# Filter layer of a Hyena block: two matmul passes on both partition halves, magnitude sums on TensorE, half of the spectrum sums on VectorE

## The chip, the cores and the metric

The kernel runs on one core of a Trainium2 chip. The metric is device time in microseconds of one execution, lower is better. Before the change three executions took 3139.27, 3143.67 and 3150.66 us; the median is 3143.67 us.

## What is computed

One inference step of a two-layer network for 1024 latent tokens and 128 context tokens, model width 1024: layer 0 is differential attention, layer 1 a bidirectional Hyena long convolution, each followed by a SwiGLU feed-forward part. The change touches only the filters of the long convolution, which don't depend on the tokens:

```python
def implicit_filter(L, w1, b1, w2, b2, w3, b3, freq):
    ...
    hdn = jnp.sin(fr * (z @ w1.astype(f32) + b1.astype(f32)))
    hdn = jnp.sin(fr * (hdn @ w2.astype(f32) + b2.astype(f32)))
    h = (hdn @ w3.astype(f32) + b3.astype(f32)).reshape(L, 2, D_MODEL)
    ...
    h = h * jnp.exp(-t[:, None, None] * deltas)
    return h / (jnp.sum(jnp.abs(h), axis=(0, 1), keepdims=True) + FILT_EPS)
```

`z` are 33 features of each position, the hidden width is 64, and `h` holds a forward and a backward filter for each of the 1024 channels. The convolution is done through spectra; the filter's own spectrum is computed by matmuls with a table of cosines and sines. Everything is float32.

## The kernel before

Matmuls take operands of a reduced float32 type. To keep float32 accuracy an operand x is split into a high part, x rounded to that type (a copy on ScalarE), and a low part, x minus the high part (a subtraction). `three` (L304) then adds three products: high x high, high x low, low x high. Its matmuls are lines L305, L306 and L307, and nearly every matmul of the kernel has one of these lines; so the profile tells them apart by tiles. In the same way `tt` (L1248) is the line of most elementwise operations, on VectorE or, if told so, on GpSimd (POOL in the profile).

**filters (L1280)** runs first, before the attention layer. It loads the features and small weights on SyncE's queue, makes two sine layers (`sine`, L1264, seven VectorE instructions, then Sin on ScalarE), and gets `hid`: 64 hidden rows and a row of ones for the bias, by 1152 positions (1024 + 128). L1322 and L1323 split it into `hids`, high and low. The table of cosines and sines is loaded and split next (`forward_table`). Then a loop goes over 8 channel tiles of 128 channels. In it stand side by side the spectrum of tile ct, the filter in time of tile ct + 1, the weights of tile ct + 2, and a few steps of unrelated work (`start` and `early_ada`: adaLN weights from DRAM with one-row matmuls at L368, and the normalisation of the input in three chunks, the results being `hh` and `hl`). When the loop is done, the projection of the attention layer (`qk`, L544) begins.

**filter_weights (L1356)** loads decay tables and the 65 x 2 x 128 weights of a tile (64 rows and a bias row, forward and backward), forms their sum and difference on GpSimd (L1367, L1368), and splits them (ScalarE L1369, GpSimd L1370) into `wh` and `wl` (tiles wsh and wsl in the profile).

**filter_time (L1373)** makes the filter of 9 position blocks: three matmuls each of 65 rows by 256 columns into `mm` banks of PSUM, then VectorE multiplies by the decay into `filt`. For the sum of magnitudes ScalarE takes absolute values (L1399, L1400), VectorE the larger of the two (L1402, since |a + b| and |a - b| have max |a| + |b|), then a TENSOR_REDUCE over the 8 blocks (L1403), and two one-column matmuls against a vector of ones (L1408) sum over partitions. Row 0 of the filter is repaired on GpSimd (L1414, L1415; tile nsq, then filt). `hilo` splits the filter into the operands of the spectrum (ScalarE L1393, VectorE L1394 by way of L1249; the tiles share the names wh and wl).

**filter_spectrum (L1423)** is called twice for a tile. Four matmul groups (`dft`, L1351, with the table th, tl) give PSUM banks; ScalarE copies one operand to SBUF, VectorE makes four sums and differences `f` with one operand in PSUM, and GpSimd four sums and differences `K` of 256 columns from `f` (L1444 to L1447; both tiles are called bf). K goes to DRAM.

The order of instructions on each engine is not the program's: a list scheduler with a cost model orders them when the kernel is built, within the dependences. `issue_after` (L1326, L1334) holds ScalarE's instructions of the block behind the last Sin.

Of the kernel before, what the change touches and what calls it, by code (L numbers as in the profile page):

```python
# [9 lines left out]
F32 = mybir.dt.float32  # L10
F32R = mybir.dt.float32r
AF = mybir.ActivationFunctionType
ALU = mybir.AluOpType
AX = mybir.AxisListType
ENG = mybir.EngineType

P = 128
# [4 lines left out]
NT = LS + LP  # L22
# [83 lines left out]
SUB = HALF // 2  # L106
# [44 lines left out]
class Net:  # L151
# [1096 lines left out]
    def tt(self, o, a, b, op, eng=None):  # L1248
        (eng or self.nc.vector).tensor_tensor(out=o, in0=a, in1=b, op=op)  # L1249
# [30 lines left out]
    def filters(self):  # L1280
        nc, i, sp = self.nc, self.i, self.sp
        H, N = NT // 2, NT // 4
        w1 = self.tl(sp, [33, 64], tag="fw1")
        w2 = self.tl(sp, [P, 64], tag="fw2")
        vec = self.tl(sp, [P, 3], tag="fvec")
        zf = self.htile([33, NT])
        nc.sync.dma_start(zf, i["k_zfeat"])
        nc.sync.dma_start(w1, i["fw1"])
        for r in (0, 64):
            nc.sync.dma_start(w2[r : r + 64], i["fw2"])  # L1290
            nc.sync.dma_start(vec[r : r + 64], i["fvec"])
        hid = self.tl(sp, [65, NT], tag="filt", bufs=2)
        nc.vector.memset(hid[64:65], 1.0)
        mid = self.tl(sp, [P, H], tag="bf", bufs=3)
        cols = [slice(N * q, N * q + N) for q in range(2)]
        xs = []
        for q, c in enumerate(cols):
            ps = self.aux()
            for r in (0, 64):
                nc.tensor.matmul(  # L1300
                    ps[r : r + 64, :N], w1, zf[:, H * (r // 64) + N * q :][:, :N], start=True, stop=True, tile_position=(0, r)
                )
            xs.append(self.sine([ps[:, :N]], vec, 0))
        for c, x in zip(cols, xs):
            mark = nc.scalar.activation(mid[:, c], x, AF.Sin)
        xs = []
        for c in cols:
            halves = []
            for r in (0, 64):
                ps = self.mm()  # L1310
                nc.tensor.matmul(
                    ps[0:64, :N], w2[r : r + 64], mid[r : r + 64, c], start=True, stop=True, tile_position=(r, 0)
                )
                halves.append(ps[0:64, :N])
            xs.append(self.sine(halves, vec, 1))
        for c, x in zip(cols, xs):
            for k in range(2):
                mark = nc.scalar.activation(hid[0:64, H * k + c.start : H * k + c.stop], x[:, N * k : N * k + N], AF.Sin)
        hids = [self.tl(sp, [65, NT], F32R, tag="hid" + n) for n in "hl"]
        for q in range(2):  # L1320
            c = slice(H * q, H * q + H)
            nc.scalar.activation(hids[0][:, c], hid[:, c], AF.Copy)  # L1322
            nc.vector.tensor_tensor(out=hids[1][:, c], in0=hid[:, c], in1=hids[0][:, c].bitcast(F32), op=ALU.subtract)  # L1323
        self.forward_table(sp, sp, "filt")
        self.d_w = [self.tl(self.dp, [P, 2, P], F32, f"d_w{c}") for c in range(KT)]
        with self.tc.issue_after(mark.ins):  # L1326
            w = [self.filter_weights(0), self.filter_weights(1)]
        cur = self.filter_time(0, hids, w.pop(0))
        rest, ada = self.start(), self.early_ada()
        next(rest)  # L1330
        for _ in cur:
            pass
        for ct in range(KT):
            with self.tc.issue_after(mark.ins):  # L1334
                for _ in range(PACE):
                    next(rest, None)
            z = self.zs
            if ct + 2 < KT:
                w.append(self.filter_weights(ct + 2))
            nxt = self.filter_time(ct + 1, hids, w.pop(0)) if ct + 1 < KT else iter(())  # L1340
            next(nxt, None)
            for _ in range(AHEAD.count(ct)):
                next(ada, None)
            self.filter_spectrum(ct, 0, *z[0])
            next(nxt, None)
            self.filter_spectrum(ct, 1, *z[1])
            next(nxt, None)
        for _ in rest:
            pass
# [6 lines left out]
    def filter_weights(self, ct):  # L1356
        nc, i, sp, tt = self.nc, self.i, self.sp, self.tt
        dec = self.tl(self.wp, [P, 8, P], tag="raw", bufs=2)
        nc.sync.dma_start(dec, i["k_decay"][ct][:, 0:LS].rearrange("p (a c) -> p a c", a=8))
        decp = self.tl(self.np_, [P, P], tag="ndg", bufs=2)  # L1360
        nc.sync.dma_start(decp, i["k_decay"][ct][:, LS : LS + P])
        w3 = self.tl(sp, [65, 2, P], tag="w3", bufs=2)
        nc.sync.dma_start(w3, i["fw3"][ct])
        wsd = self.tl(sp, [65, 2, P], tag="wsd", bufs=1)
        wh = self.tl(sp, [65, 2, P], F32R, tag="wsh", bufs=2)
        wl = self.tl(sp, [65, 2, P], F32R, tag="wsl", bufs=2)
        tt(wsd[:, 0], w3[:, 0], w3[:, 1], ALU.add, nc.gpsimd)  # L1367
        tt(wsd[:, 1], w3[:, 0], w3[:, 1], ALU.subtract, nc.gpsimd)  # L1368
        nc.scalar.activation(wh, wsd, AF.Copy)  # L1369
        tt(wl, wsd, wh.bitcast(F32), ALU.subtract, nc.gpsimd)  # L1370
        return dec, decp, wh, wl

    def filter_time(self, ct, hid, w):  # L1373
        nc, i, sp, tt = self.nc, self.i, self.sp, self.tt
        ADD, SUB, MUL = ALU.add, ALU.subtract, ALU.mult
        dec, decp, wh, wl = w
        filt = self.tl(sp, [P, 9, 2, P], tag="filt", bufs=2)
        for a0 in range(0, 9, 2):
            m = min(2, 9 - a0)
            ps = self.mm()  # L1380
            for a in range(m):
                out = ps[:, 256 * a : 256 * a + 256].rearrange("p (f c) -> p f c", f=2)
                t = slice(P * (a0 + a), P * (a0 + a) + P)
                self.three(out, hid[0][:, t], hid[1][:, t], wh, wl)
            d = dec[:, a0 : a0 + m] if m == 2 else decp.unsqueeze(1)
            tt(filt[:, a0 : a0 + m], ps[:, : 256 * m].rearrange("p (a f c) -> p a f c", a=m, f=2), d.unsqueeze(2).to_broadcast([P, m, 2, P]), MUL)
        sm = self.tl(sp, [P, 2, P], tag="fsum", bufs=1)
        self.zs = []

        def hilo(part):  # L1390
            zh = self.tl(self.wp, [P, 8, P], F32R, tag="wh", bufs=3)
            zl = self.tl(self.wp, [P, 8, P], F32R, tag="wl", bufs=3)
            nc.scalar.activation(zh, filt[:, 0:8, part], AF.Copy)  # L1393
            tt(zl, filt[:, 0:8, part], zh.bitcast(F32), SUB)  # L1394
            self.zs.append((zh, zl))

        am = self.tl(self.wp, [P, 8, P], tag="wh", bufs=3)
        am2 = self.tl(self.wp, [P, 8, P], tag="wl", bufs=3)
        nc.scalar.activation(am, filt[:, 0:8, 0], AF.Abs)  # L1399
        nc.scalar.activation(am2, filt[:, 0:8, 1], AF.Abs)  # L1400
        yield
        tt(am, am, am2, ALU.max)  # L1402
        nc.vector.tensor_reduce(out=sm[:, 0], in_=am.rearrange("p a c -> p c a"), axis=AX.X, op=ADD)  # L1403
        nc.scalar.activation(am2[:, 0:2], filt[:, 8], AF.Abs)
        tt(sm[:, 1], am2[:, 0], am2[:, 1], ALU.max)
        ps = self.aux()
        for g in range(2):
            nc.tensor.matmul(ps[:, g : g + 1], sm[:, g], self.ones[:, 0:1], start=True, stop=True)  # L1408
        den = self.den[:, ct]
        nc.vector.tensor_scalar(out=den, in0=ps[:, 0:2], scalar1=FILT_EPS, scalar2=None, op0=ADD)  # L1410
        nc.vector.reciprocal(den, den)
        row = filt[0:1].rearrange("p (u a) f c -> p u a f c", u=1)[:, 0, 0:9:8]
        t = self.tl(self.np_, [1, 2, P], tag="nsq", bufs=2)
        tt(t, row[:, :, 0], row[:, :, 1], ADD, nc.gpsimd)  # L1414
        nc.gpsimd.tensor_scalar(  # L1415
            out=row, in0=t.unsqueeze(2).to_broadcast([1, 2, 2, P]), scalar1=0.5, scalar2=1.0, op0=MUL, op1=MUL
        )
        nc.scalar.dma_start(self.d_w[ct], filt[:, 8])
        hilo(0)
        yield  # L1420
        hilo(1)

    def filter_spectrum(self, ct, part, zh, zl):  # L1423
# [17 lines left out]
        X1 = X1.rearrange("p (a b) -> p a b", a=2)  # L1441
        tt(f[:, 2], X1[:, part], s[:, part], ADD)
        tt(f[:, 3], X1[:, 1 - part], s[:, 1 - part], SUB)
        tt(K[:, 0], f[:, 0], f[:, 2], ADD, nc.gpsimd)  # L1444
        tt(K[:, 2], f[:, 0], f[:, 2], SUB, nc.gpsimd)
        tt(K[:, 1], f[:, 1], f[:, 3], SUB if part else ADD, nc.gpsimd)
        tt(K[:, 3], f[:, 1], f[:, 3], ADD if part else SUB, nc.gpsimd)  # L1447
        nc.scalar.dma_start(self.d_f[ct][:, part], K)
# [300 lines left out]
```

## Time and profile before

| | |
|---|---|
| median of three timed runs | 3143.67 us |
| profiled execution | 3150.18 us, span of the instructions 3148.3 us |
| TensorE busy, share of the span | 3051.0 us, 97% |
| VectorE | 1901.2 us, 60% |
| ScalarE | 1171.4 us, 37% |
| GpSimd | 962.2 us, 31% |
| stretch of the filters, until the first matmul of the projection | 182.4 us |

PE is TensorE's matmuls, PEld its weight loads, DVE VectorE, ACT ScalarE, POOL GpSimd, SP SyncE; a q behind the name is the engine's queue for DMAs. A row of a group gives line, engine, operation, out<-in tiles, shapes, count, then busy time, the mean duration of one in ns, and the idle time of the engine just before with what ended it. Matmuls are pipelined, so durations of neighbours overlap and the distance between their starts says more. PEclk is the granted clock of TensorE.

### The profile page before, as it was taken

To read this page: it belongs to the slowest core of one execution; us is meant where nothing else is said; L and a number is where in the kernel's file an instruction comes from. 1 tells how busy PE (TensorE), PEld (TensorE's weight loads), DVE (VectorE), ACT (ScalarE), POOL (GpSimd) and SP (SyncE) were. 2 spreads that over 40 slices of the span, in tenths; PEclk is the share of its full clock that TensorE was granted. 3 is DMA by queue.
4 is the path that set the end of the run, shared out by engine and by line. 5 is a ranking of instruction groups with operands and counts; after the bars stand their busy time and mean duration, and the time that the engine had idled before them with its cause. 6 is when DMAs were issued, how large, how long until landed. Compare 5 with 4: busy or idle time off the path is not lost. (4 is left out here: it accounts for less than half of the span.)

```text
span 3148.3 us, 53347 instructions
## 1 busy us (share of the span) xinstructions
PE 3051.0 (97%) x21418; PEld 2977.4 (95%) x21418; DVE 1901.2 (60%) x3111; ACT 1171.4 (37%) x2248; POOL 962.2 (31%) x842
## 2 busy tenths in 40 slices
PE   6899999999999999999999999999999999999998
PEld 5779989999999999999999999999999999999998
DVE  7866523888836645445544678886456454445555
ACT  3631123888825322222211443335643222222114
POOL 5744310444422434343000322221223343430003
PEclk9899999999999999999999999999999999999999
DMA  6665352433241222224555223345621212225311
GB/s 250 202 215 186 135 162 82 98 88 90 57 152 55 73 74 74 74 74 148 194 205 193 101 96 123 130 149 181 214 77 57 77 71 77 75 73 199 107 63 67
DMA packets 164494, 379.14 MB, mean 120 GB/s; under 512 B 17391, under 2 KB 80247, under 8 KB 161560
## 3 DMA queue, kind: packets, MB, share of 16 engines
q1 hardware_dynamic: 148872, 353.37, 34.1%
q10 hardware_dynamic: 13968, 17.65, 1.6%
q0 software_dynamic: 1408, 4.72, 0.4%
q8 instruction: 169, 2.77, 0.4%
q14 instruction: 77, 0.63, 0.1%
HBM read 278.94 MB, written 96.73 MB: 119 GB/s over the span
## 5 line engine op out<-in xcount | busy, mean ns | idle before, releaser
L306 PE MATMUL mm<-hs,wh 128*128 128x384 f32 x1632 | 548.2, 336 | 0.4 <-POOL hs L469 0.3
L307 PE MATMUL mm<-hs,wl 128*128 128x384 f32 x1632 | 546.6, 335 | 0.0
L305 PE MATMUL mm<-hs,wh 128*128 128x384 f32 x1632 | 545.9, 336 | 0.0
L863 DVE SCALAR_TENSOR_TENSOR xk<-mm,ada,xk 128x192 f32<-128x192 f32 (+3 forms) x560 | 233.2, 453 | 333.5 <-PE mm L307 328.1
L1249 DVE TENSOR_TENSOR xk<-pr,xk 128x576 f32<-128x576 f32 x200 | 150.7, 754 | 391.9 <-PE pr L307 205.9
L420 POOL TENSOR_TENSOR nacc<-nacc,nsq 128x384 f32<-128x384 f32 x104 | 118.3, 1138 | 682.4 <-ACT nsq L416 680.8
L306 PEld LDWEIGHTS mm<-hs,wh 128*128 128x128 f32 x1632 | 306.4, 188 | 4.7 <-issue 2.2
L305 PEld LDWEIGHTS mm<-hs,wh 128*128 128x128 f32 x1632 | 306.1, 188 | 3.5 <-DVE xk L863 1.8
L307 PEld LDWEIGHTS mm<-hs,wl 128*128 128x128 f32 x1632 | 306.5, 188 | 2.0 <-issue 0.6
L1634 ACT ACTIVATE wh<-raw 128x1024 fp32r<-128x1024 f32 x156 | 164.8, 1057 | 369.3 <-PE mm L306 322.3
L1249 POOL TENSOR_TENSOR xk<-xk,xk 128x576 f32<-128x576 f32 x80 | 116.6, 1457 | 543.4 <-DVE xk L1249 449.3
L1635 DVE TENSOR_TENSOR wl<-raw,wh 128x1024 fp32r<-128x1024 f32 x156 | 197.0, 1263 | 68.4 <-ACT wh L1634 68.1
L1635 DVE TENSOR_TENSOR wl<-xk,wh 128x512 fp32r<-128x512 f32 x160 | 176.9, 1144 | 52.3 <-ACT wh L1634 52.0
L305 PE MATMUL mm<-hh,wh 128*128 128x384 f32 x576 | 193.9, 340 | 2.9 <-ACT hh L527 2.3
L306 PE MATMUL mm<-hl,wh 128*128 128x384 f32 x576 | 195.0, 339 | 0.8 <-DVE hl L528 0.8
L307 PE MATMUL mm<-hh,wl 128*128 128x384 f32 x576 | 195.0, 339 | 0.0
L772 DVE TENSOR_REDUCE nm<-sc 128x1 f32<-128x1152 f32 x128 | 173.5, 1356 | 35.2 <-PE sc L766 35.1
L1048 ACT ACTIVATE xk<-xk 128x576 f32<-128x576 f32 x40 | 27.4, 686 | 363.1 <-DVE xk L1249 363.1
L774 ACT ACTIVATE pr<-sc,nm 128x1152 f32<-128x1152 f32 x128 | 156.7, 1224 | 14.8 <-DVE nm L772 9.0
L765 PE MATMUL sc<-kk,qs 128*128 128x384 f32 x384 | 140.7, 366 | 3.3 <-ACT pr L774 3.3
L791 PE MATMUL tr<-v,at 128*128 128x128 f32 x1152 | 139.4, 275 | 0.5 <-ACT at L786 0.5
L791 PEld LDWEIGHTS tr<-v,at 128*128 128x128 f32 x1152 | 133.8, 192 | 3.1 <-ACT at L786 0.8
(383 smaller groups left out, 8768.1 us busy)
## 6 DMA issues: line engine op xcount, KB each, us to landing
raw<-w_gu SPq DMA_DIRECT2D x88, 512.0 KB, 3.5
araw<-ada_w SPq DMA_DIRECT2D x64, 512.0 KB, 4.1
d_a<-xk SPq DMA_DIRECT2D x80, 288.0 KB, 2.1
raw<-w_down SPq DMA_DIRECT2D x44, 512.0 KB, 3.5
araw<-d_a SPq DMA_DIRECT2D x36, 576.0 KB, 7.3
kk<-d_k SPq DMA_DIRECT2D x16, 1152.0 KB, 8.7
raw<-w_in SPq DMA_DIRECT2D x24, 512.0 KB, 3.5
hl<-ada_w SPq DMA_DIRECT2D x23, 512.0 KB, 7.5
```

Source lines behind the costliest of these rows:

```text
L305: self.nc.tensor.matmul(out, ah, bh, start=first, stop=False, **kw)
L306: self.nc.tensor.matmul(out, ah, bl, start=False, stop=False, **kw)
L307: self.nc.tensor.matmul(out, al, bh, start=False, stop=last, **kw)
L420: nc.gpsimd.tensor_tensor(out=self.acc[c], in0=self.acc[c], in1=sq, op=ALU.add)
L765: nc.tensor.matmul(sc[:, c, :CH], lhs, kk[:, 0, p, ks], start=True, stop=False)
L772: nc.vector.tensor_reduce(out=nm, in_=sv, axis=AX.XY, op=ALU.max, negate=True)
L774: nc.scalar.activation(e.rearrange("p (a b) -> p a b", a=3), sv, AF.Exp, bias=nm, accum_out=st[hd][3][:, p, qt : qt + 1])
L791: self.nc.tensor.matmul(po[:, :P], at[:, b], v[:, b], start=b == 0, stop=b == 8)
L863: self.nc.vector.scalar_tensor_tensor(out=x, in0=ps[:, s:e], scalar=gate[:, d, g : g + 1], in1=x, op0=ALU.mult, op1=ALU.add)
L1249: (eng or self.nc.vector).tensor_tensor(out=o, in0=a, in1=b, op=op)
L1634: self.nc.scalar.activation(hi, x, AF.Copy)
L1635: (eng or self.nc.vector).tensor_tensor(out=lo, in0=x, in1=hi.bitcast(F32), op=ALU.subtract)
```

## The change

The filter's matmul takes two passes. `w2` is loaded twice side by side, so that the second sine layer gives the 64 hidden rows twice, on partitions 0 to 63 and 64 to 127. The first operand, `both`, has their high part in the lower half and the low part in the upper; it meets `wh`, in which the high part of the weights stands in both halves. The second, `plus`, has the high part of the hidden rows and, below, 33 rows of ones; it meets `wl` with the low part of the weights and, on rows 64 and 96, the high and low part of the bias. The weights of a tile are loaded in four DMAs to two fixed tiles, and sum, difference and split are made for this form.

The reduction over the 8 blocks and its tile fsum go: eight one-column matmuls accumulate the blocks in PSUM in its place. Of the four K sums, two go from GpSimd to VectorE.

```diff
--- before.py
+++ after.py
@@ -1281,16 +1281,16 @@
         nc, i, sp = self.nc, self.i, self.sp
         H, N = NT // 2, NT // 4
         w1 = self.tl(sp, [33, 64], tag="fw1")
-        w2 = self.tl(sp, [P, 64], tag="fw2")
+        w2 = self.tl(sp, [P, 2, 64], tag="fw2")
         vec = self.tl(sp, [P, 3], tag="fvec")
         zf = self.htile([33, NT])
         nc.sync.dma_start(zf, i["k_zfeat"])
         nc.sync.dma_start(w1, i["fw1"])
         for r in (0, 64):
-            nc.sync.dma_start(w2[r : r + 64], i["fw2"])
+            for u in range(2):
+                nc.sync.dma_start(w2[r : r + 64, u], i["fw2"])
             nc.sync.dma_start(vec[r : r + 64], i["fvec"])
-        hid = self.tl(sp, [65, NT], tag="filt", bufs=2)
-        nc.vector.memset(hid[64:65], 1.0)
+        hid = self.tl(sp, [P, NT], tag="filt", bufs=2)
         mid = self.tl(sp, [P, H], tag="bf", bufs=3)
         cols = [slice(N * q, N * q + N) for q in range(2)]
         xs = []
@@ -1309,18 +1309,26 @@
             for r in (0, 64):
                 ps = self.mm()
                 nc.tensor.matmul(
-                    ps[0:64, :N], w2[r : r + 64], mid[r : r + 64, c], start=True, stop=True, tile_position=(r, 0)
+                    ps[:, :N], w2[r : r + 64].rearrange("p a b -> p (a b)"), mid[r : r + 64, c], start=True, stop=True, tile_position=(r, 0)
                 )
-                halves.append(ps[0:64, :N])
+                halves.append(ps[:, :N])
             xs.append(self.sine(halves, vec, 1))
         for c, x in zip(cols, xs):
             for k in range(2):
-                mark = nc.scalar.activation(hid[0:64, H * k + c.start : H * k + c.stop], x[:, N * k : N * k + N], AF.Sin)
-        hids = [self.tl(sp, [65, NT], F32R, tag="hid" + n) for n in "hl"]
+                mark = nc.scalar.activation(hid[:, H * k + c.start : H * k + c.stop], x[:, N * k : N * k + N], AF.Sin)
+        both, plus = (self.tl(sp, [P, NT], F32R, tag="hid" + n) for n in "hl")
+        nc.vector.memset(plus[64:97].bitcast(F32), 1.0)
+        hids = both, plus[0:97]
+        self.w3 = [self.tl(sp, [P, 2, 2, P], tag=f"w3{n}") for n in range(2)]
+        for t in self.w3:
+            nc.gpsimd.memset(t[:, 1], 0.0)
         for q in range(2):
             c = slice(H * q, H * q + H)
-            nc.scalar.activation(hids[0][:, c], hid[:, c], AF.Copy)
-            nc.vector.tensor_tensor(out=hids[1][:, c], in0=hid[:, c], in1=hids[0][:, c].bitcast(F32), op=ALU.subtract)
+            nc.scalar.activation(both[:, c], hid[:, c], AF.Copy)
+            nc.scalar.activation(plus[0:64, c], hid[0:64, c], AF.Copy)
+            nc.vector.tensor_tensor(
+                out=both[64:P, c], in0=hid[64:P, c], in1=both[64:P, c].bitcast(F32), op=ALU.subtract
+            )
         self.forward_table(sp, sp, "filt")
         self.d_w = [self.tl(self.dp, [P, 2, P], F32, f"d_w{c}") for c in range(KT)]
         with self.tc.issue_after(mark.ins):
@@ -1359,15 +1367,21 @@
         nc.sync.dma_start(dec, i["k_decay"][ct][:, 0:LS].rearrange("p (a c) -> p a c", a=8))
         decp = self.tl(self.np_, [P, P], tag="ndg", bufs=2)
         nc.sync.dma_start(decp, i["k_decay"][ct][:, LS : LS + P])
-        w3 = self.tl(sp, [65, 2, P], tag="w3", bufs=2)
-        nc.sync.dma_start(w3, i["fw3"][ct])
-        wsd = self.tl(sp, [65, 2, P], tag="wsd", bufs=1)
-        wh = self.tl(sp, [65, 2, P], F32R, tag="wsh", bufs=2)
-        wl = self.tl(sp, [65, 2, P], F32R, tag="wsl", bufs=2)
-        tt(wsd[:, 0], w3[:, 0], w3[:, 1], ALU.add, nc.gpsimd)
-        tt(wsd[:, 1], w3[:, 0], w3[:, 1], ALU.subtract, nc.gpsimd)
-        nc.scalar.activation(wh, wsd, AF.Copy)
-        tt(wl, wsd, wh.bitcast(F32), ALU.subtract, nc.gpsimd)
+        w3 = self.w3[ct % 2]
+        for r in (0, 64):
+            nc.sync.dma_start(w3[r : r + 64, 0], i["fw3"][ct][0:64])
+        for r in (64, 96):
+            nc.sync.dma_start(w3[r : r + 1, 1], i["fw3"][ct][64:65])
+        ws = self.tl(sp, [P, 2, P], tag="wsd", bufs=1)
+        wh = self.tl(sp, [P, 2, P], F32R, tag="wsh", bufs=2)
+        wl = self.tl(sp, [97, 2, P], F32R, tag="wsl", bufs=2)
+        tt(ws, w3[:, :, 0], w3[:, :, 1], ALU.add, nc.gpsimd)
+        tt(w3[:, :, 1], w3[:, :, 0], w3[:, :, 1], ALU.subtract, nc.gpsimd)
+        for n, y in enumerate((ws, w3[:, :, 1])):
+            nc.scalar.activation(wh[:, n], y[:, 0], AF.Copy)
+            nc.scalar.activation(wl[64:97, n], y[64:97, 1], AF.Copy)
+            tt(wl[0:64, n], y[0:64, 0], wh[0:64, n].bitcast(F32), ALU.subtract, nc.gpsimd)
+            tt(wl[96:97, n], y[96:97, 1], wl[96:97, n].bitcast(F32), ALU.subtract, nc.gpsimd)
         return dec, decp, wh, wl
 
     def filter_time(self, ct, hid, w):
@@ -1381,10 +1395,10 @@
             for a in range(m):
                 out = ps[:, 256 * a : 256 * a + 256].rearrange("p (f c) -> p f c", f=2)
                 t = slice(P * (a0 + a), P * (a0 + a) + P)
-                self.three(out, hid[0][:, t], hid[1][:, t], wh, wl)
+                nc.tensor.matmul(out, hid[0][:, t], wh, start=True, stop=False)
+                nc.tensor.matmul(out, hid[1][:, t], wl, start=False, stop=True)
             d = dec[:, a0 : a0 + m] if m == 2 else decp.unsqueeze(1)
             tt(filt[:, a0 : a0 + m], ps[:, : 256 * m].rearrange("p (a f c) -> p a f c", a=m, f=2), d.unsqueeze(2).to_broadcast([P, m, 2, P]), MUL)
-        sm = self.tl(sp, [P, 2, P], tag="fsum", bufs=1)
         self.zs = []
 
         def hilo(part):
@@ -1400,12 +1414,13 @@
         nc.scalar.activation(am2, filt[:, 0:8, 1], AF.Abs)
         yield
         tt(am, am, am2, ALU.max)
-        nc.vector.tensor_reduce(out=sm[:, 0], in_=am.rearrange("p a c -> p c a"), axis=AX.X, op=ADD)
         nc.scalar.activation(am2[:, 0:2], filt[:, 8], AF.Abs)
-        tt(sm[:, 1], am2[:, 0], am2[:, 1], ALU.max)
+        sm = am2[:, 2]
+        tt(sm, am2[:, 0], am2[:, 1], ALU.max)
         ps = self.aux()
-        for g in range(2):
-            nc.tensor.matmul(ps[:, g : g + 1], sm[:, g], self.ones[:, 0:1], start=True, stop=True)
+        for a in range(8):
+            nc.tensor.matmul(ps[:, 0:1], am[:, a], self.ones[:, 0:1], start=a == 0, stop=a == 7)
+        nc.tensor.matmul(ps[:, 1:2], sm, self.ones[:, 0:1], start=True, stop=True)
         den = self.den[:, ct]
         nc.vector.tensor_scalar(out=den, in0=ps[:, 0:2], scalar1=FILT_EPS, scalar2=None, op0=ADD)
         nc.vector.reciprocal(den, den)
@@ -1441,8 +1456,8 @@
         X1 = X1.rearrange("p (a b) -> p a b", a=2)
         tt(f[:, 2], X1[:, part], s[:, part], ADD)
         tt(f[:, 3], X1[:, 1 - part], s[:, 1 - part], SUB)
-        tt(K[:, 0], f[:, 0], f[:, 2], ADD, nc.gpsimd)
-        tt(K[:, 2], f[:, 0], f[:, 2], SUB, nc.gpsimd)
+        tt(K[:, 0], f[:, 0], f[:, 2], ADD)
+        tt(K[:, 2], f[:, 0], f[:, 2], SUB)
         tt(K[:, 1], f[:, 1], f[:, 3], SUB if part else ADD, nc.gpsimd)
         tt(K[:, 3], f[:, 1], f[:, 3], ADD if part else SUB, nc.gpsimd)
         nc.scalar.dma_start(self.d_f[ct][:, part], K)
```

## Prediction

> **What bounds the kernel now.** The run of the profile took 3150.18 us (span 3148.3 us and 1.88 us around it); the median of the three timed runs, 3143.67 us, is 6.5 us lower. I work out a change against the profiled execution and then take the same change off the median. I began with the granted clock, then cut the span into stretches around the filter layer, the only part that the diff touches, then read the groups of each engine in that stretch, then single durations.
>
> ```profile
> core 0: 3148.3 us, clock 0.988
> core 0: us, PE busy (x) PEld busy (x) DVE busy (x) ACT busy (x) POOL busy (x), PEclk, DMA share, GB/s
> 0.00:25.39 25.39, 4.37 (x16) 1.61 (x17) 17.09 (x37) 5.59 (x13) 6.62 (x10) 1.00 0.89 311
> 25.39:46.70 21.31, 20.79 (x187) 18.75 (x187) 16.87 (x19) 7.18 (x12) 12.36 (x12) 1.00 0.96 362
> 46.70:182.40 135.70, 119.50 (x995) 101.37 (x992) 118.77 (x191) 75.38 (x136) 98.31 (x116) 0.92 0.52 176
> L305 PE MATMUL mm<-hh,wh x115: 331/334/689, 182.4 to 259.8; 128*128 128x384 f32 x115
> ```
>
> Over the whole span the kernel is TensorE's, but this change lives in the first 182 us: the first matmul of the projection after the filters (last row: duration ns minimum, median, maximum, then first and last start) starts at 182.4, and none earlier. So the filter layer is a stage of its own, and whatever makes it shorter moves the rest forward one for one. In its long stretch, 46.70 to 182.40, no engine is full: TensorE 119.50 of 135.70 us (88%), VectorE 118.77 (88%), GpSimd 98.31 (72%). Two engines at 88% take turns at being last, and they wait for each other. That is why a saving on one of them comes out at less than its size.
>
> ```profile
> L1249 DVE TENSOR_TENSOR wl<-filt,wh 128x1024 fp32r<-128x1024 f32 x16 | 35.6, 2248 | 2.4 <-POOL nacc L420 1.4 <-ACT wh L1393 1.0
> L1403 DVE TENSOR_REDUCE fsum<-wh 128x128 f32<-128x1024 f32 x8 | 16.3, 2040 | 0.1
> L1249 DVE TENSOR_TENSOR fsum<-wl 128x128 f32<-128x128 f32 x8 | 4.9, 616 | 0.0
> L1249 POOL TENSOR_TENSOR bf<-bf 128x256 f32<-128x256 f32 x58 | 48.0, 853 | 16.3 <-issue 11.0 <-DVE bf L1249 4.8 <-POOL bf L1249 0.5
> L305 PE MATMUL mm<-wsh,hidh 65*128 65x256 f32 x72 | 24.2, 336 | 16.3 <-ACT hidh L1322 12.7 <-DVE bf L1249 3.6
> PE mm L305 <- DVE filt L1249: 6.0, 3, 3.3
> ACT wh L1393 <- POOL filt L1415: 8.6, 6, 4.2
> ```
>
> These are groups (busy time, mean ns) and two waits. The edited work is here: the sum of magnitudes (L1403, 16.3 us of VectorE), the spectrum sums (bf<-bf, GpSimd's largest group, 58 of the 64 inside this stretch) and the 3 x 72 matmuls of the filter in time.
>
> **The change part by part.**
>
> *Sum of magnitudes.* Eight reductions leave VectorE: 8 x 2.04 = -16.3 us. The second small sum (fsum<-wl) stays, with another name for its place. On TensorE a tile has 9 one-column matmuls in place of 2.
>
> ```profile
> 60.85 0.28 PE L305 MATMUL mm<-wsh,hidh 65*128 65x256 f32 x1
> 60.97 0.28 PE L306 MATMUL mm<-wsl,hidh 65*128 65x256 f32 x1
> 26.20 0.41 PE L306 MATMUL mm<-wsl,hidh 65*128 65x256 f32 x1
> 26.41 0.41 PE L305 MATMUL mm<-wsh,hidh 65*128 65x256 f32 x1
> 98.62 0.50 PE L1408 MATMUL aux<-ones,fsum 128*128 128x1 f32 x4
> 99.05 0.64 PE L368 MATMUL aux<-hl,cs 128*32 128x128 f32 x16
> ```
>
> Matmul records overlap, so I price TensorE by the distance between starts. The two sums of one tile show as four records, so a matmul of this kind is two records; four of them take 99.05 - 98.62 = 0.43 us, 0.107 each. Seven more matmuls in each of 8 tiles: 7 x 2 x 8 x 0.107 = +12.0 us of TensorE.
>
> *Two passes for three.* Nine matmuls less in each tile, 72 in all. A filter matmul takes 0.12 us at the full rate (60.85 to 60.97) and 0.21 in the first stretch (26.20 to 26.41). The number of rows of the contraction (65 before, 128 and 97 after) changes neither: the 128-row spectrum matmuls of 256 columns follow each other at the same distance in the stretch (46.94 and 47.06 below). The first two tiles are made in the slow part: 18 x 0.21 = -3.8 us. The other six: 54 x 0.12 = -6.5 us. With the +12.0 of the sums TensorE has 5.5 us more to do after its start, not less. It is idle for 16.2 us of the long stretch, so part of this falls into gaps: bounds -6.5 (all sums in gaps) and +5.5 (none), taken +2.5.
>
> ```profile
> 46.94 0.28 PE L306 MATMUL mm<-tl,wh 128*128 128x256 f32 x1
> 47.06 0.28 PE L307 MATMUL mm<-th,wl 128*128 128x256 f32 x1
> L1249 DVE TENSOR_TENSOR bf<-mm,xs x64: 404/410/425, 54.1 to 186.0; 128x256 f32<-128x256 f32 x64
> L1249 POOL TENSOR_TENSOR bf<-bf x64: 715/732/1795, 58.7 to 189.2; 128x256 f32<-128x256 f32 x64
> L1249 DVE TENSOR_TENSOR wl<-filt,wh x16: 1210/1764/6703, 38.3 to 175.9; 128x1024 fp32r<-128x1024 f32 x16
> L1249 DVE TENSOR_TENSOR fsum<-wl x8: 274/488/1628, 37.3 to 173.7; 128x128 f32<-128x128 f32 x8
> L1403 DVE TENSOR_REDUCE fsum<-wh x8: 2000/2038/2103, 35.4 to 171.8; 128x128 f32<-128x1024 f32 x8
> ```
>
> *Spectrum sums.* Of four sums in each half spectrum, two move from GpSimd to VectorE: 32 instructions. On GpSimd they cost 32 x 0.853 = -27.3 us. No row shows this shape from SBUF alone on VectorE. The uncontended ends of two neighbours, 0.274 us for 128 elements and 1.210 for 1024, give 0.41 for 256 by a straight line, the same as with one operand in PSUM (0.410): 32 x 0.41 = +13.1 us. So VectorE alone would gain 16.3 - 13.1 = 3.2 us.
>
> But look at minimum, median and maximum. Operations with one operand in PSUM are flat (404 to 425), the reduction too (2000 to 2103). Those with both operands in SBUF are not: 1.21 to 6.70, 0.27 to 1.63, and GpSimd's own 0.715 to 1.795. They get into each other's way. The excess is (2.248 - 1.210) x 16 + (0.616 - 0.274) x 8 = 19.3 us already. The change takes out an operation that never waits and puts in 32 that may. The Trainium skill says as much (SBUF — State Buffer, "Who interferes with whom"): a VectorE instruction with two SBUF inputs and a GpSimd instruction that reads SBUF exclude each other, and the one that issues second waits for the whole of the first. The rows above agree, and by that rule, with GpSimd first each time, the sum would be that of the slower rival below.
>
> For the price: GpSimd starts its two sums of a half spectrum just when VectorE starts its own. At best VectorE goes first (0), at worst it stands behind one of them (0.715) per pair: 16 x 0.715 = 11.4 us. Nothing in the rows decides who is first; I take the middle, +5.7. Against it, GpSimd has less to do, so that present collisions shrink. Its new load is the weights:
>
> ```profile
> L1249 POOL TENSOR_TENSOR wsd<-w x13: 447/455/1434, 25.2 to 105.2; 65x128 f32<-65x128 f32 x13
> L1249 POOL TENSOR_TENSOR wsl<-wsd,wsh x7: 722/741/1486, 26.3 to 123.7; 65x256 fp32r<-65x256 f32 x7
> L1249 POOL TENSOR_TENSOR nsq<-filt x8: 717/731/1702, 32.4 to 165.4; 1x256 f32<-1x256 f32 x8
> ```
>
> One row of 256 elements costs as much as 65 or 128 rows (0.717, 0.722, 0.715), so elements per row count alone. A tile had 2 x 0.45 + 0.72 = 1.6 us; it gets 2 x 0.72 (sum and difference, with the biases beside) and 4 x 0.45 (low parts), 3.2 us: +1.6 x 8 = +13 us. GpSimd ends 14 us shorter, 13% of some 111 us in the two stretches; 13% of 19.3 gives -2.5. VectorE: -16.3 + 13.1 + 5.7 - 2.5 = 0.
>
> *GpSimd's own waits.* ScalarE waits 8.6 us for the repair of row 0 on GpSimd (L1415) before it can round the filter. A GpSimd with fewer sums reaches it earlier: 0 to -8.6, taken half, -4.3.
>
> *ScalarE.* A tile's rounding of weights goes from one instruction of 0.406 us to four short ones; with 0.273 us for 128 elements that is 1.1, +5.5 us in all, at no cost: ScalarE is busy 75.38 of 135.70 us, and the weights are made two tiles ahead. Without that cover they would cost the 5.5.
>
> *The start.*
>
> ```profile
> L1369 ACT ACTIVATE wsh<-wsd 65x256 fp32r<-65x256 f32 x8 | 3.2, 406 | 2.2 <-POOL bf L1249 1.2 <-PE mm L307 1.0
> L377 ACT ACTIVATE ndg<-aux 128x128 f32<-128x128 f32 x8 | 2.2, 273 | 11.9 <-PE aux L368 6.6 <-POOL bf L1249 5.3
> 2.19 0.59 SPq L1291 DMA_DIRECT2D fvec<-fvec  x1
> 2.82 0.60 SPq L1290 DMA_DIRECT2D fw<-fw  x1
> 5.50 1.20 DVE L1272 TENSOR_SCALAR xs<-aux,fvec 128x288 f32<-128x288 f32 x2 [0.45 <-DMA fvec<-fvec]
> 25.37 1.59 DVE L1323 TENSOR_TENSOR hidl<-filt,hidh 65x576 fp32r<-65x576 f32 x2 [2.55 <-ACT hidh L1322]
> 37.41 0.59 PE L1408 MATMUL aux<-ones,fsum 128*128 128x1 f32 x2
> ```
>
> Two more loads of fw2 are put ahead of the second fvec load on SyncE's queue, at 0.63 us apiece: the sine chain on VectorE, which waits for fvec, starts 1.2 us later. Six more loads of weights (three each for tiles 0 and 1) stand ahead of x and of the adaLN weights on the same queue, at most 3.8 us; the DMA share of 0.89 and 0.96 says that enough is queued before them, so 0 to 3.8, taken 0.5. The first matmul now needs the low part in the same operand: half of 1.59 us of VectorE, +0.8, before the first pass; before, two products went ahead of it. Against these stand the -3.8 of TensorE up to 37.41, of which I count half, since VectorE's multiplications then follow at their own pace: 1.2 + 0.5 + 0.8 - 1.9 = +0.6.
>
> **Sum:** 0.6 + 2.5 + 0 - 4.3 = -1.2 us, 3149.0 for the profiled execution, 3142.5 against the median. A measurement of this kernel can tell some 0.3% (9.4 us) from no change; this is well inside.
>
> **The rivals.** *Faster.* VectorE goes first in every pair, the sums by TensorE fall into its gaps and GpSimd's repair is never late. TensorE and VectorE being equal, the longer saving doesn't add to the shorter: -6.5 at most for the two, -8.6 for the repair and 0 at the start: -15, 3128.6. For it speaks that 16.2 us of TensorE idle time are there, and that the reduction stands just ahead of the low part of the spectrum's operand. Against it, that VectorE has nearly the same instructions' time as before.
>
> *Slower.* The two engines collide. Its place is the end of each half spectrum; its price is -3.2 + 11.4 = +8.2 on VectorE, and as VectorE then holds back the operand of the next matmuls, TensorE's added 5.5 no longer hides: +13.7 less the 2.5 of relief, +11, 3154.8. It decides from a mean excess of (3.2 + 2.5) / 32 = 0.18 us per moved sum; the two-operand VectorE groups of now have (19.3 / 24) 0.8, which speaks for it. GpSimd's shorter queue speaks against it.
>
> *Nothing where it was meant.* The pass that is left out lay in TensorE's waits and the reduction in VectorE's; then all terms but the start vanish, +0.6: inside the same band, and counted there.
>
> **How the numbers follow.** The forecast (with the last rival) has 0.53, faster by over 0.3% 0.28, slower by over 0.3% 0.19: gains have one more path (three engines can each release another), and the collision needs both engines at once. The range goes from the faster case, 3129, to the slower, 3154, which leaves the rest beyond both.
>
> **What would show it.** Right: the first matmul of the projection within 5 us of 182.4; the moved sums on VectorE with a minimum near 410 ns and a mean near 0.6 us; 18 records of one column per tile about 0.1 us apart; GpSimd some 14 us less busy; ScalarE's wait for the repair down by half. A mean of the moved sums near 410 ns with that matmul before 173 would be the faster rival, a mean of 0.8 us and that matmul after 191 the slower. I am wrong altogether if the time moves behind the projection's start, for instance because the third chunk of x is normalised at another time.

## The result, and the profile after

The changed kernel takes 3172.98 us (median of five runs, 3167.4 to 3182.0); it is slower, 1.0088 times the kernel before, 95% interval 1.0072 to 1.0104, or about 28 us. The forecast was 3142.5, and the range ended at 3154. Times here and below are medians and the ratios are those of the fast runs alone (one run of e1_early_write, 6038 us, and one of e6_before_kdve, 3342 us, are not in them), so differences of the two can come apart by a few us. The profiled execution took 3172.98 us, with a span of 3171.2 us against 3148.3.

The same views as in the prediction, of the changed kernel. First the clock, then the three stretches up to the projection (busy time of each engine, granted clock, DMA share), then when the spectrum matmuls (tile th) and the projection (tile hh) start for the first and last time. `kernel.py` has other line numbers behind the edits: the first pass of the filter is L1398, the sums L1422.

```profile
core 0: 3171.2 us, clock 0.983
0.00:25.00 25.00, 4.54 (x16) 2.23 (x16) 14.89 (x36) 6.25 (x15) 5.30 (x13) 1.00 0.78 258
25.00:46.00 21.00, 4.52 (x18) 3.99 (x18) 3.54 (x3) 4.19 (x11) 7.58 (x9) 1.00 0.97 372
62.60:213.00 150.40, 135.96 (x1111) 117.80 (x1112) 114.54 (x223) 81.87 (x153) 84.12 (x97) 0.85 0.48 166
L305 PE MATMUL mm<-th,wh x128: 277/393/628, 62.6 to 212.3; 128*128 128x256 f32 x64, 128*128 128x512 f32 x64
L305 PE MATMUL mm<-hh,wh x123: 334/334/689, 213.0 to 299.9; 128*128 128x384 f32 x123
```

The second row of stretches is the surprise. Between 25 and 46 us the kernel before had TensorE busy for 20.79 of 21.31 us (25.39 to 46.70); now it is 4.52 of 21.00, and VectorE 3.54. The first spectrum matmul comes at 62.6 instead of 46.7 us (+15.9), the projection at 213.0 instead of 182.4 (+30.6). The delay stays: the last matmul of the group mm<-hh,wh starts at 1007.8 instead of 978.2 us, 29.6 later. That the span grew by only 22.9 is in good part the choice of runs, for the profiled run before was 6.5 us above its median.

Who waited, in the timelines of TensorE, VectorE and GpSimd:

```profile
47.99 0.55 PE L1398 MATMUL mm<-wsh,hidh 128*128 128x256 f32 x1 [17.82 <-ACT wsh L1381]
44.26 2.80 DVE L485 TENSOR_TENSOR tl<-filt,th 128x2048 fp32r<-128x2048 f32 x1 [16.65 <-POOL th L484]
42.32 1.90 POOL L484 TENSOR_SCALAR th<-filt 128x2048 fp32r<-128x2048 f32 x1 [12.82 <-DMA filt<-k_fwd]
47.15 2.48 DVE L1249 TENSOR_TENSOR filt<-mm,raw 128x512 f32<-128x512 f32 x4
```

Begin with the last row. The multiplications that empty the PSUM banks (47.15) stand in VectorE's queue behind the split of the spectrum table (44.26), which waits for GpSimd (42.32), which waits for the table's load, tile filt from k_fwd. TensorE has filled its banks and stands still for 17.8 us; that the row names ScalarE's wsh is the nearest event, not the cause: wsh of that tile was rounded by 27.8. The multiplications have a second reason to wait, by the code: the filter that they write has the tag filt as well, and all tiles of this tag share two buffers. With both halves of the table in them, the first to come free is that of the split that ends at 47.06; the rows can't tell this wait from the place in VectorE's queue. SyncE's queue shows why the table is late. In the kernel before, and after it:

```profile
4.11 0.59 SPq L1256 DMA_DIRECT2D filt<-k_fwd  x1
8.00 0.38 SPq L493 DMA_DIRECT2D hl<-xt  x1
24.05 0.33 SPq L1256 DMA_DIRECT2D filt<-k_fwd  x1
```

```profile
11.23 0.40 SPq L493 DMA_DIRECT2D hl<-xt  x1
12.30 4.11 SPq L502 DMA_DIRECT2D hh<-ada_w  x3
25.49 2.89 SPq L502 DMA_DIRECT2D hl<-ada_w  x3
31.88 0.33 SPq L1256 DMA_DIRECT2D filt<-k_fwd  x1
38.35 0.35 SPq L1256 DMA_DIRECT2D filt<-k_fwd  x1
```

The first half of the table was the first large load on the queue, at 4.11 us; now it is behind x and twelve loads of adaLN weights (six of them in the rows), at 31.88. The diff doesn't touch `forward_table`. It does drop one line, `nc.vector.memset(hid[64:65], 1.0)`, the row of ones in hid. Hid and the two halves of the raw table take their buffers from the same two of tag filt, and hid's turn comes first. That memset was hid's first write, at 1.58 us; without it the first write is the Sin of the second layer, at 19.76 us, and the load of the table is ordered after it.

### The profile page after: what moved, and what is told of

Its sections match the earlier page's. It is cut to its first block, busy times and chain, and to the rows that moved or that the text cites. A ratio compares the mean times of both kernels' runs of the same rounds, so it can differ in the third digit from the quotient of the medians.

```text
span 3171.2 us, 53565 instructions
## 1 busy us (share of the span) xinstructions
PE 3057.1 (96%) x21458; PEld 2987.0 (94%) x21458; DVE 1890.7 (60%) x3135; ACT 1179.2 (37%) x2274; POOL 952.4 (30%) x836
```

## The experiments

Theory A says that this lost early write is the cause. Theory B is the slower rival of the prediction: the loop itself, by collisions of the moved sums and by the matmuls of the magnitudes. All times are compared with the kernel before on the same chip (medians of 3145.2 to 3146.5 us there).

**The early write, put back and taken away.**

```diff
 # e1_early_write: the changed kernel, and
         hid = self.tl(sp, [P, NT], tag="filt", bufs=2)
+        nc.vector.memset(hid[64:65], 1.0)
```

> The changed kernel with one VectorE memset of row 64 of hid put back ahead of everything, so that hid has its buffer of tag filt early and the first half of the spectrum table can be loaded at once into the other one. Theory A (the lost early write put the table's loads behind x and the adaLN weights on SyncE's queue; the parts named in the change are about neutral): the first spectrum matmul, 62.6 us after the change, comes back to 46 to 50, the projection starts at 180 to 190 instead of 213, time 3135 to 3150. Theory B (the loop itself became slower: the moved sums meet GpSimd at the shared port and TensorE has the one-column sums to do): the start recovers, but the loop keeps its 150 us instead of 136, the projection starts near 197, time 3155 to 3162.

Measured: 3154.69 us, 1.0024 (1.0014 to 1.0035). First spectrum matmul at 49.8, projection at 196.3 us.

```diff
 # e2_before_late_write: the kernel before, and
-        hid = self.tl(sp, [65, NT], tag="filt", bufs=2)
-        nc.vector.memset(hid[64:65], 1.0)
+        hid = self.tl(sp, [64, NT], tag="filt", bufs=2)
...
+        for t, x in zip(hids, (1.0, 0.0)):
+            nc.vector.memset(t[64:65].bitcast(F32), x)
...
-            nc.scalar.activation(hids[0][:, c], hid[:, c], AF.Copy)
+            nc.scalar.activation(hids[0][0:64, c], hid[:, c], AF.Copy)
```

(and likewise the subtraction).

> The kernel before with only its early write of hid taken away: the row of ones is put straight into the two split operands (1 in the high one, 0 in the low one), so that the first Sin is the first writer of hid. Nothing else of the change is in it. Theory A: the table's loads fall behind x and the adaLN weights as in the changed kernel, the first spectrum matmul at 58 to 65, time 3160 to 3175. Theory B: the start is at most 16 us later and the loop keeps its 136 us, so that at most 3160 and likely less than 3155, since part of the later start is made good by loads that have landed by then.

Measured: 3169.36 us, 1.0067 (1.0054 to 1.0079). First spectrum matmul at 61.1, projection at 201.9 us. SyncE's queue of e1_early_write, then of e2_before_late_write:

```profile
5.51 0.59 SPq L1256 DMA_DIRECT2D filt<-k_fwd  x1
14.60 0.40 SPq L493 DMA_DIRECT2D hl<-xt  x1
15.72 2.18 SPq L1256 DMA_DIRECT2D filt<-k_fwd  x1
```

```profile
7.15 0.38 SPq L493 DMA_DIRECT2D hl<-xt  x1
30.59 0.33 SPq L1256 DMA_DIRECT2D filt<-k_fwd  x1
33.20 0.33 SPq L1256 DMA_DIRECT2D filt<-k_fwd  x1
```

One memset moves the table's load from 31.88 to 5.51 us in the one kernel, and its absence from 4.11 to 30.59 in the other. The first spectrum matmul moves by 12.8 and 14.4 us with it. In time it is worth 0.0064 in the first (about 20 us) and 0.0067 in the second (about 21 us). Theory A holds for some 20 of the 28 us. But e1_early_write is still 0.24% (7.6 us) above the kernel before, its time above theory A's bounds (3150), and its projection starts where theory B had it (near 197): for the rest there is theory B.

**Parts taken back, with the early write kept.** Both go from e1_early_write.

```diff
 # e3_early_kpool
-        tt(K[:, 0], f[:, 0], f[:, 2], ADD)
-        tt(K[:, 2], f[:, 0], f[:, 2], SUB)
+        tt(K[:, 0], f[:, 0], f[:, 2], ADD, nc.gpsimd)
+        tt(K[:, 2], f[:, 0], f[:, 2], SUB, nc.gpsimd)
```

> As e1_early_write, with all four spectrum sums on GpSimd as before. Theory A: within 5 us of e1_early_write. Theory B (collisions of the moved sums): 6 to 12 us faster than e1_early_write, and the loop shorter by as much.

```diff
 # e4_early_reduce
-        for a in range(8):
-            nc.tensor.matmul(ps[:, 0:1], am[:, a], self.ones[:, 0:1], start=a == 0, stop=a == 7)
...
+        nc.vector.tensor_reduce(out=sm[:, 1], in_=am.rearrange("p a c -> p c a"), axis=AX.X, op=ADD)
```

> As e1_early_write, with the sum of magnitudes over the eight blocks by a reduction on VectorE as before (in a spare part of the same tile) and two one-column matmuls. Theory A: within 5 us of e1_early_write, to either side. Theory B with the one-column matmuls as its cause: 5 to 10 us faster than e1_early_write.

Measured: e3_early_kpool 3151.02 us, 1.0006 (0.9996 to 1.0015), not to be told from the kernel before; e4_early_reduce 3164.88, 1.0054 (1.0042 to 1.0067). Moving the two spectrum sums to VectorE costs 0.0018, 5.7 us, just under what theory B said. The reduction put back costs 9 us, against both theories: given the rest of the change, the sums by TensorE are a gain. The reduction of e4_early_reduce isn't quite that of before: it stands behind the small maximum and writes beside it, into the tile of the absolute values. What this costs no run shows.

**Parts alone.**

```diff
 # e5_before_pesum: the kernel before with the sums by TensorE (the new lines of filter_time)
 # e6_before_kdve: the kernel before with K[:, 0] and K[:, 2] on VectorE
 # e8_two_pass_only: e4_early_reduce with all K sums on GpSimd
```

> The kernel before with one part of the change alone: the magnitudes summed over the eight blocks by eight one-column matmuls, the reduction gone. If parts add up, the 10 us between e4_early_reduce and e1_early_write are its gain (the reduction's 16.3 us on VectorE weigh more than the 12 us of matmuls): 3134 to 3141. If what a part is worth hangs on the order that the scheduler makes of the whole, this can come out anywhere from 3138 to 3155. By the working of the prediction (-16.3 on VectorE against +12.0 on TensorE, both nearly full) about 3142 to 3146.

> The kernel before with one part of the change alone: two of the four spectrum sums on VectorE. VectorE then has 13 us more and no reduction taken from it. Parts that add up: 4 to 6 us slower than before (e1_early_write against e3_early_kpool), 3150 to 3153. The rival, that the freed GpSimd repairs row 0 of the filter sooner: 3140 to 3146.

> The two-pass filter alone, with the early write of hid: reduction on VectorE and all four spectrum sums on GpSimd as before. Parts that add up: the two passes cost 11 us (e3_early_kpool has them with the sums by TensorE, which gain 9, and is 2 us above before), 3155 to 3160. If instead the two passes save what the prediction counted (10 us of TensorE, less some 4 at the start): 3138 to 3146.

Measured: e5_before_pesum 3152.31 us, 1.0020 (1.0011 to 1.0029); e6_before_kdve 3150.74, 1.0022 (1.0013 to 1.0031); e8_two_pass_only 3157.27, 1.0042 (1.0030 to 1.0055). The moved K sums cost about the same here as there, 0.0022 and 0.0018. The other two parts don't add up: each alone costs time (6 and 13 us), both together cost 2; the 13 are those of e8_two_pass_only, whose reduction has the form of e4_early_reduce.

The rows of the K sums in e6_before_kdve, on VectorE and on GpSimd (minimum, median, maximum), then two groups of e1_early_write (busy time, mean), the K sums on VectorE and the low part of the filter:

```profile
L1249 DVE TENSOR_TENSOR bf<-bf x32: 404/846/1942, 58.3 to 187.7; 128x256 f32<-128x256 f32 x32
L1249 POOL TENSOR_TENSOR bf<-bf x32: 716/776/1277, 58.7 to 188.8; 128x256 f32<-128x256 f32 x32
L1249 DVE TENSOR_TENSOR bf<-bf 128x256 f32<-128x256 f32 x32 | 23.1, 759 | 1.4 <-POOL bf L1249 1.4
L1249 DVE TENSOR_TENSOR wl<-filt,wh 128x1024 fp32r<-128x1024 f32 x16 | 22.2, 1402 | 5.1 <-ACT wh L1408 5.1
```

The minimum of 404 is the 0.41 us of the straight line. The mean of 759 lies 0.35 us above it, 11 us in all, which fits collisions with GpSimd. VectorE gains 16.3 us (the reduction) and is given 23.1 (32 x 0.759 = 24.3, overlaps counted twice). Yet it is less busy as a whole, 1895.1 us over the span for 1901.2 before: the low part of the filter, which took 35.6 us before (2248 ns each), takes 22.2. It takes 24.3 us in e6_before_kdve, where only the K sums were moved, and 21.8 in e3_early_kpool, where none was; so how often the two engines meet hangs on the order of the whole, and the busy time of VectorE doesn't tell where the time went.

**SyncE's queue.** The change brings four weight loads a tile for one.

```diff
 # e9_e3_queue: e3_early_kpool, the fvec loads ahead of the fw2 loads, and
+        q = nc.sync if ct < 2 else nc.scalar
-            nc.sync.dma_start(w3[r : r + 64, 0], i["fw3"][ct][0:64])
+            q.dma_start(w3[r : r + 64, 0], i["fw3"][ct][0:64])
```

(and the bias rows).

> As e3_early_kpool, with the two fvec loads ahead of the four fw2 loads, and the weight loads of tiles 2 to 7 (four a tile) on ScalarE's queue in place of SyncE's. If what the two passes lose is SyncE's longer queue (the first of the early adaLN loads is issued at 90 to 94 us instead of 77, and TensorE waits for these loads at 121 and 144): 5 to 10 us faster than e3_early_kpool, 3137 to 3144, with those waits under 1 us. If it is the weights' work on GpSimd and ScalarE or the granted clock: within 3 us of e3_early_kpool.

Measured: 3172.73 us, 1.0088 (1.0074 to 1.0102), 0.0082 slower than e3_early_kpool and outside both expectations. ScalarE now stands still for what its own queue has to issue, and TensorE behind it (timeline of TensorE):

```profile
42.50 0.80 PE L1401 MATMUL mm<-wsh,hidh 128*128 128x256 f32 x2 [10.85 <-ACT wsh L1384]
```

ScalarE's timeline shows what wsh (L1384) stood behind, the weight loads that it has to issue itself:

```profile
27.65 0.67 ACT L1330 ACTIVATE hidl<-filt 64x576 fp32r<-64x576 f32 x1
36.94 0.53 ACTq L1375 DMA_DIRECT2D w<-fw  x1
38.22 0.47 ACTq L1377 DMA_DIRECT2D w<-fw  x1
39.50 0.47 ACTq L1375 DMA_DIRECT2D w<-fw  x1
40.78 0.23 ACTq L1377 DMA_DIRECT2D w<-fw  x1
41.06 0.31 ACT L1384 ACTIVATE wsh<-wsd 128x128 fp32r<-128x128 f32 x1 [12.74 <-DMA hl<-ada_w]
```

The first of four issues comes 8.6 us after hidl has ended; wsh follows the last by 0.05 us. What the row names as the end of the wait, a load of adaLN weights, is only the event that came last; what else the first issue waited for the rows don't say. So this run doesn't tell whether the longer queue on SyncE costs anything; it shows that a queue with work behind it was a worse place for the loads here.

**The one-column matmuls and the clock.** In the loop the granted clock is 0.92 before and 0.85 to 0.87 in e1, e3 and e5. Of the loop's seven bursts of sums in e3_early_kpool, five have a stretch at half the clock that begins inside the burst or at most 1.4 us behind it and lasts 3.4 or 6.8 us. The first of them, in TensorE's timeline:

```profile
73.33 1.84 PE L1423 MATMUL aux<-ones,wh 128*128 128x1 f32 x16
75.04 0.36 PE L1424 MATMUL aux<-ones,wl 128*128 128x1 f32 x2
75.26 0.81 PE L435 MATMUL aux<-ones,nacc 128*128 128x1 f32 x6
77.06 0.28 PE L306 MATMUL mm<-tl,wh 128*128 128x256 f32 x1
77.18 0.28 PE L307 MATMUL mm<-th,wl 128*128 128x256 f32 x1
78.45 0.41 PE L305 MATMUL mm<-th,wh 128*128 128x256 f32 x1
78.66 0.41 PE L306 MATMUL mm<-tl,wh 128*128 128x256 f32 x1
```

Between 70.7 and 82 us TensorE has no gap over 0.7 us. After 2.6 us of matmuls that stream one column each, matmuls of 256 columns go from 0.12 us apart (77.06, 77.18) to 0.21 (78.45, 78.66). The clock is as low in e4 (0.85) and e8 (0.87), whose sums take 4 records a tile; there the stretches begin in or just behind waits of TensorE. So a wait is one way to half the rate, and the question is whether these bursts are another. The test leaves the order and the count of instructions nearly as they are and streams 128 columns of ones in place of one:

```diff
 # e14_e3_wide; the same edit on e5_before_pesum is e15_e5_wide, on e1_early_write e17_e1_wide
-            nc.tensor.matmul(ps[:, 0:1], am[:, a], self.ones[:, 0:1], start=a == 0, stop=a == 7)
-        nc.tensor.matmul(ps[:, 1:2], sm, self.ones[:, 0:1], start=True, stop=True)
+            nc.tensor.matmul(ps[:, 0:P], am[:, a], self.ones, start=a == 0, stop=a == 7)
+        nc.tensor.matmul(ps[:, P : 2 * P], sm, self.ones, start=True, stop=True)
...
-        nc.vector.tensor_scalar(out=den, in0=ps[:, 0:2], scalar1=FILT_EPS, scalar2=None, op0=ADD)
+        nc.vector.tensor_scalar(out=den, in0=ps[:, P - 1 : P + 1], scalar1=FILT_EPS, scalar2=None, op0=ADD)
```

> As e3_early_kpool, but the matmuls that sum the magnitudes run against all 128 columns of ones instead of one; the first of the equal result columns is read. Theory C: a burst of one-column matmuls (18 records in 1.8 to 2 us) counts as idleness for TensorE's clock, since half-rate stretches begin within some 5 us of most such bursts in e3_early_kpool and e5_before_pesum; with 128 columns they go, 100 ns a record being bound by the weight load anyway: 4 to 10 us faster than e3_early_kpool (3138 to 3144), granted clock of the loop above 0.92 instead of 0.87. Rival D (the half rate comes from waits of TensorE, whatever its matmuls): within 3 us of e3_early_kpool or slower by what more columns cost, 72 x 2 records x up to 0.03 us = 4 us, and the clock as before.

> As e5_before_pesum (the kernel before with the sums by TensorE alone), with 128 columns of ones. Theory C: 6 to 14 us faster than e5_before_pesum (3138 to 3146), since there the half-rate stretches after the bursts are longest; granted clock of the loop from 0.85 to above 0.91. Rival D: within 4 us of e5_before_pesum.

> As e1_early_write (the whole change with the early write of hid), with 128 columns of ones. Theory C: 4 to 10 us faster than e1_early_write, 3144 to 3150. Rival D: within 4 us of e1_early_write.

Measured: e14_e3_wide 3145.28 us, 0.9998 (0.9989 to 1.0007); e15_e5_wide 3149.26, 1.0008 (0.9999 to 1.0017); e17_e1_wide 3151.48, 1.0023 (1.0014 to 1.0032). The loops, first spectrum matmul to projection, of e3_early_kpool and e14_e3_wide, then of e5_before_pesum and e15_e5_wide (each fence one kernel):

```profile
49.70:193.20 143.50, 133.97 (x1111) 115.94 (x1111) 96.12 (x192) 80.82 (x159) 113.92 (x138) 0.87 0.50 175
```

```profile
49.60:187.60 138.00, 124.99 (x1111) 106.86 (x1111) 97.86 (x192) 79.61 (x157) 112.90 (x137) 0.95 0.53 182
```

```profile
45.60:196.90 151.30, 143.04 (x1165) 124.61 (x1166) 115.39 (x194) 79.06 (x143) 102.81 (x120) 0.85 0.48 166
```

```profile
45.50:189.80 144.30, 131.49 (x1164) 112.92 (x1165) 114.73 (x193) 76.49 (x137) 101.38 (x120) 0.95 0.52 177
```

The same burst in e14_e3_wide, and matmuls behind it:

```profile
70.59 1.95 PE L1423 MATMUL aux<-ones,wh 128*128 128x128 f32 x16
72.38 0.39 PE L1424 MATMUL aux<-ones,wl 128*128 128x128 f32 x2
75.25 0.28 PE L305 MATMUL mm<-th,wh 128*128 128x256 f32 x1
75.37 0.28 PE L306 MATMUL mm<-tl,wh 128*128 128x256 f32 x1
```

The number of matmul records is the same but for one, and the clock goes from 0.87 to 0.95 and from 0.85 to 0.95; the loops are 5.5 and 7.0 us shorter. Behind the burst the matmuls stay 0.12 us apart, and the three half-rate stretches that are left in the loop of e14_e3_wide each begin within 2 us of the end of a wait of TensorE of 1.8 to 3.8 us. That is theory C, for the clock. In the time it shows as 0.0008 and 0.0012 (2.5 and 3.8 us), with intervals that overlap, and with the whole change, e17_e1_wide, as 0.0001; all three are within what rival D allowed, so the time alone decides nothing. In e17_e1_wide the clock of the loop is 0.92, and the K sums on VectorE still hold the loop at 141.9 us (48.3 to 190.2) against the 138.0 of e14_e3_wide, where all of them are on GpSimd and the clock is 0.95.

**Fewer loads.**

```diff
 # e16_one_load_wide: e14_e3_wide with the operands laid out in DRAM as they stand in SBUF
-        for r in (0, 64):
-            nc.sync.dma_start(w3[r : r + 64, 0], i["fw3"][ct][0:64])
-        for r in (64, 96):
-            nc.sync.dma_start(w3[r : r + 1, 1], i["fw3"][ct][64:65])
+        nc.sync.dma_start(w3, i["fw3"][ct])
```

(fw2 and fvec in one load each, too).

> A candidate: as e14_e3_wide, with the weights of a tile, the fw2 and the fvec loads each laid out beforehand so that one DMA does for four, four and two (the rows of zeros come from DRAM, too). SyncE's queue is then shorter than before the change. If the start and the queue are what the two passes still lose: 3 to 8 us faster than e14_e3_wide and, with theory C, below the kernel before (3130 to 3142). If not: within 3 us of e14_e3_wide.

Measured: 3145.29 us, 0.9999 (0.9990 to 1.0007), the same as e14_e3_wide. The first spectrum matmul is at 45.4 us, 4 us earlier than there, but its loop, at a clock of 0.91 for 0.95, takes 144.2 us for 138.0, and nothing is left at the end. No version here beats the kernel before.

## Why the prediction was wrong

*The start* is the step that failed: "1.2 + 0.5 + 0.8 - 1.9 = +0.6". The first spectrum matmul came 15.9 us later. The deleted memset is in none of the terms, so it was put at nothing: I never asked what else than a row of ones it did. It fixed when a shared buffer is first taken, and by that the place of two large loads on a queue. By the experiments this alone moves the first spectrum matmul by 12.8 us (62.6 to 49.8) and 14.4 us (46.7 to 61.1) and the time by 20 and 21 us, where the whole change costs 28. The pieces that were counted were nearer. The sine chain starts at 6.79 us instead of 5.50 (1.3 for 1.2), the first matmul of the filter in e1_early_write at 27.8 instead of 25.4 (2.4 for 2.0), and its first spectrum matmul 3.1 us later for the +0.6; the -1.9 doesn't show. The prediction counted the loads that new loads move back on SyncE's queue; it should have asked, too, which loads wait for a buffer of the tag of each tile whose first write changes.

*The moved spectrum sums*: the price on VectorE was right at its low end (404 to 407 ns for 410) and the collision higher than the middle (0.35 us a sum in the place of 0.18). What the move costs is shown by four pairs that differ in nothing else: +0.0012 (e8 to e4), +0.0018 (e3 to e1), +0.0022 (before to e6) and +0.0025 (e14 to e17), 4 to 8 us; the intervals of the last two pairs are apart, those of the first two overlap. It fits the slower rival, at half to all of its price on VectorE, 8.2, and e1_early_write has both of that rival's signs, a mean of 0.76 us and the projection after 191 us (196.3). That the collision costs it, and not the plain 13.1 us of more work on VectorE, is argued: no run has the one without the other. The relief, counted at 2.5 us, was 11.3 in e6_before_kdve for the low part of the filter alone (35.6 to 24.3). The exclusion that the Trainium skill states (SBUF — State Buffer, "Who interferes with whom") agrees with these rows: the sums with one operand in PSUM (bf<-mm) stay at 406 to 426 ns in e1_early_write.

*Sum of magnitudes and two passes*: 18 records a tile and about 0.1 us each were right (1.71 us for 16 in e3), and the sum of the two parts with the early write is +2 us, not to be told from none; counted on TensorE were bounds of -6.5 and +5.5. That each alone costs 6 and 13 us doesn't fit a sum of durations. Part of it is the clock, above. The remainder stays open: every edit gives the scheduler another order, and no run here holds the order fixed while it takes a part out.

*GpSimd* is 9.8 us less busy over the span (962.2 to 952.4), 14 were counted. ScalarE's wait for the repair of row 0 in the filter layer is 5.7 us instead of 8.6: counted -4.3, got -2.9, and it is small beside the rest.

*"Moves the rest forward one for one"* holds for the changed kernel, 30.6 us later at the projection's start and 29.6 at 978 us, but not for smaller delays. In e5_before_pesum the projection starts 14.5 us later and the first matmul of the group mm<-wh,hh 6.9 later (418.3 for 411.4); in e3_early_kpool it is 10.8 and 5.3. What makes up for the rest no run takes apart. The 7 us that the clock gave back from e5 to e15 are 2.6 at that matmul; the 5.5 from e3 to e14 are 5.5 in the spans, too, so their 2.5 by the ratio isn't explained by this.

## What to carry to other kernels

When a line goes, ask what it ordered, not only what it computed: the first write of a tile in a rotating set of buffers can decide when an unrelated load of the same tag is issued, and a look at the order on the DMA queues of both kernels shows it at once. A tile's two-operand SBUF work moved from GpSimd to VectorE costs its lone duration only at the minimum; price it with the mean of such groups that are there already, and expect that mean to move with the order. In a stage with two engines near 90%, test parts by pairs that differ in one edit and don't add up parts that were measured alone.

## What the hardware showed that was not expected

Matmuls with one moving column seem to count as idleness for TensorE's clock. The burst shown (2.6 us, with no gap) is followed, 1.4 us behind it, by 3.4 us of matmuls at half the rate; behind others the slow stretch lasts 3.4 or 6.8 us. And the same bursts with 128 columns bring the loop's granted clock from 0.87 and 0.85 to 0.95 at 0.1 us a record as before (16 records take 1.79 us for 1.71). The Trainium skill (TensorE: Matmul & The Clock Gate, "Part 1: The HAM clock gate") has the clock halved after an idle window of some 3.4 us; the rows here show it halved with no gap over 0.7 us in TensorE's issuing, which points to the amount streamed, and not the presence of instructions, as what counts in this case.

On GpSimd a row of 128 elements costs 0.45 us for one partition as for 64 (wsl on row 96 against rows 0 to 63, in the changed kernel), as the prediction took it from 256 elements.
